# Strassen's multiplication, one level, for the gate and up products of four SwiGLU FFNs

## Chip, cores and metric

The kernel runs on one core of a Trainium2 chip. The metric is the device time of one execution in microseconds (us), read as the median of several runs. The engines have queues of their own: PE (TensorE, matrix products; PEld are its weight loads), DVE (VectorE), ACT (ScalarE), POOL (GpSimd), and SP (SyncE, which issues the DMAs of the weights). Each engine works its queue in order.

## The reference, cut

Two transformer blocks follow one another on 512 tokens of 1024 features, in float32. The second one has two layers, each with a SwiGLU FFN before its mixer and one behind it, so four in all, with 2816 hidden features (`D_FF`):

```python
def swiglu(h, w_gate, w_up, w_down):
    return (jax.nn.silu(h @ w_gate) * (h @ w_up)) @ w_down
...
    for layer in range(DEPTH):
...
        x = x + 0.5 * swiglu(rmsnorm_2(x, ffn1_norm[layer]), ffn1_w_gate[layer],
                             ffn1_w_up[layer], ffn1_w_down[layer])
...
        x = x + 0.5 * swiglu(rmsnorm_2(x, ffn2_norm[layer]), ffn2_w_gate[layer],
                             ffn2_w_up[layer], ffn2_w_down[layer])
```

## The kernel before

**Precision.** Every float32 factor is split into a high part (a copy to the matmul type) and a low part (the factor less its high part), and a product is three matmuls: high by high, high by low, low by high. Weights are split on the core: ACT writes the high part (line 78, tile `wh`), DVE the low one (line 79, `wl`). Activations are kept feature-major, `xT` [128, 8, 512], with the split parts `ah` and `al`.

**The four FFNs** are called "a", "b", "c", "d" here. Their hidden features are 22 chunks of 128. For a chunk m, the gate block (1024 x 128) is the stationary side in 8 pieces of 128x128, the tokens move: 8 x 3 matmuls of 512 columns (`fm`, lines 252, 254, 256), and the same for up. That makes 1056 such matmuls in an FFN. Then DVE multiplies both by `rB` (the norm's factor for each token, lines 394 and 396), ACT takes Silu (395), POOL multiplies (397), and `split` makes the parts `hh` (ACT, 237) and `hl` (DVE, 238). `rB` comes from a chain behind the first gate product (`stat1`, `stat2`; the matmuls of line 301, the copy of line 302).

**Down products** come in four groups of 6, 6, 5 and 5 chunks (`GROUPS`), each with 8 requests, one for each 128 output features: three matmuls of 512 columns for a chunk (lines 364 to 366), 528 in an FFN, and an addition to `xT` on DVE (369). A group is emitted behind the first chunk of the next group.

**The weights' queue** (`Stream`) is one list of requests for the whole kernel. SP loads a request into one of three staging tiles `ws`; when request i is fetched, the requests up to i + 2 are split, so that a weight's high and low parts are emitted two requests ahead of the matmuls that read them. The order of all work is that of emission.

Of the kernel before, what the change touches and what calls it, by code (L numbers as in the profile page):

```python
# [32 lines left out]

VECS = (
# [14 lines left out]
class Stream:  # L49
    def __init__(self, nc, pool, nst, nhl):  # L50
        self.nc, self.pool, self.nst, self.nhl = nc, pool, nst, nhl
        self.req, self.i, self.nd, self.ns = [], 0, 0, 0
        self.st, self.hl = {}, {}

    def add(self, key, ap, raw=False, use=None):
        """a request; its parts are high and low ones, or itself if raw, or what use(tile) makes of it."""
        self.req.append((key, ap, raw, use))

    def _dma(self, j):
        ap = self.req[j][1]  # L60
        a, b = ap.shape[1], ap.shape[2]
        t = self.pool.tile([P, 1024], F32, tag="ws", bufs=self.nst, name=f"ws{j}")
        v = t[:, :a * b].rearrange("p (a b) -> p a b", b=b)
        self.nc.sync.dma_start(v, ap)
        self.st[j] = (t, a, b)

    def _split(self, j):
        t, a, b = self.st.pop(j)
        n = a * b
        if self.req[j][3]:  # L70
            self.hl[j] = self.req[j][3](t[:, :n].rearrange("p (a b) -> p a b", b=b))
            return
        if self.req[j][2]:
            self.hl[j] = t[:, :n].rearrange("p (a b) -> p a b", b=b)
            return
        h = self.pool.tile([P, 1024], F32R, tag="wh", bufs=self.nhl, name=f"wh{j}")
        l = self.pool.tile([P, 1024], F32R, tag="wl", bufs=self.nhl, name=f"wl{j}")
        self.nc.scalar.activation(h[:, :n], t[:, :n], AF.Copy)  # L78
        self.nc.vector.tensor_tensor(l[:, :n], t[:, :n], h[:, :n], ALU.subtract)  # L79
        self.hl[j] = tuple(z[:, :n].rearrange("p (a b) -> p a b", b=b) for z in (h, l))  # L80
# [37 lines left out]
class Kernel:  # L118
    def __init__(self, tc, I, es):
# [94 lines left out]
    def vcols(self, first):  # L214
        """rows to columns: VC[:, i] is row i."""
# [27 lines left out]
    def fm(self, outs, w, x, nk=NK, k0=0, kw=0, first=True, last=True):  # L243
        """outs: [(psum AP, column slice of x)]; w: hi/lo [128, k, 128] stationary."""
# [13 lines left out]
    def fm_side(self, jobs, x, hook):  # L258
        """fm's side by side, chunk of x by chunk as they come, by parts of the tokens (the outs of a job)."""
# [7 lines left out]
    # ---- norms over the feature axis of a feature-major tensor  # L267
# [10 lines left out]
    def rcols(self, acc, nt, eps=EPS, dim=D, tag="M"):  # L278
        """acc [128, nt*128] per-partition partial sums of squares -> [128, nt] rsqrt columns."""
# [24 lines left out]
    # ---- block 2  # L304
# [17 lines left out]
    def feed(self, d, n, stats=True):  # L322
        """chunk n of x is final: its scaled hi/lo parts and its squares."""
# [15 lines left out]

    def plan_swiglu(self, key, wg, wu, wd):  # L340
        for gi, (m0, nm) in enumerate(GROUPS):
            for m in range(m0, m0 + nm):
                self.ws.add((key, "g", m), colblock(wg, m * P))
                self.ws.add((key, "u", m), colblock(wu, m * P))
                if m == m0 and gi:
                    self.plan_down(key, gi - 1, wd)
        self.plan_down(key, 3, wd)
# [8 lines left out]
    def down512(self, key, gi, hs, scale, on_x=None):  # L356
        nc = self.nc
        m0, nm = GROUPS[gi]
        for n in range(NK):
            wh, wl = self.ws.get((key, "d", gi, n))  # L360
            q = self.mps()
            for k in range(nm):
                hh, hl = hs[m0 + k]
                nc.tensor.matmul(q, wh[:, k], hh[:, :T], start=k == 0, stop=False)  # L364
                nc.tensor.matmul(q, wh[:, k], hl[:, :T], start=False, stop=False)  # L365
                nc.tensor.matmul(q, wl[:, k], hh[:, :T], start=False, stop=k == nm - 1)  # L366
            x = self.xT[:, n]
            s = scale if isinstance(scale, float) else scale(n)
            nc.vector.scalar_tensor_tensor(x, q, s, x, ALU.mult, ALU.add)  # L369
            if on_x is not None and gi == 3:  # L370
                on_x(n)

# [5 lines left out]
    def swiglu(self, key, d, on_x):  # L378
        nc = self.nc
        hs = {}  # L380
        sl = slice(0, T)
        for gi, (m0, nm) in enumerate(GROUPS):
            for m in range(m0, m0 + nm):
                q = self.dbl()
                w = self.ws.get((key, "g", m))
                self.fm([(q[:, 0], sl)], w, d.x)
                if d.rB is None:
                    self.stat1(d)
                w = self.ws.get((key, "u", m))
                self.fm([(q[:, 1], sl)], w, d.x)  # L390
                if d.rB is None:
                    self.stat2(d)
                a, b = self.tmp(T, tag="ta"), self.tmp(T, tag="tb")
                nc.vector.tensor_tensor(a, q[:, 0], d.rB, ALU.mult)  # L394
                nc.scalar.activation(a, a, AF.Silu)  # L395
                nc.vector.tensor_tensor(b, q[:, 1], d.rB, ALU.mult)
                nc.gpsimd.tensor_tensor(b, a, b, ALU.mult)  # L397
                hs[m] = self.htiles()
                self.split(hs[m][0], hs[m][1], b)
# [2069 lines left out]
```

## Time and profile before

| | us |
|---|---|
| median of 3 runs (3926.29 to 3926.95) | 3926.34 |
| span of the profiled execution, first to last instruction | 3923.9 |
| PE busy in it | 3757.1 |
| DVE busy in it | 2155.4 |
| ACT busy in it | 1375.5 |
| FFN "a", 1920.5 to 2297.4 | 376.9 |
| FFN "b", 2484.9 to 2860.6 | 375.7 |
| FFN "c", 2953.3 to 3326.6 | 373.3 |
| FFN "d", 3539.2 to 3912.5 | 373.3 |

The profile is of one execution, whose span is 2.4 us shorter than the median. An FFN's stretch runs from its first gate matmul to its last down matmul. Matmuls overlap in the records: the start of one to the start of the next is what it costs, and the duration shown is longer.

### The profile page before, as it was taken

To read this page: it belongs to the slowest core of one execution; us is meant where nothing else is said; L and a number is where in the kernel's file an instruction comes from. 1 tells how busy PE (TensorE), PEld (TensorE's weight loads), DVE (VectorE), ACT (ScalarE), POOL (GpSimd) and SP (SyncE) were. 2 spreads that over 40 slices of the span, in tenths; PEclk is the share of its full clock that TensorE was granted. 3 is DMA by queue.
4 is the path that set the end of the run, shared out by engine and by line. 5 is a ranking of instruction groups with operands and counts; after the bars stand their busy time and mean duration, and the time that the engine had idled before them with its cause. 6 is when DMAs were issued, how large, how long until landed. Compare 5 with 4: busy or idle time off the path is not lost.

```text
span 3923.9 us, 48420 instructions
## 1 busy us (share of the span) xinstructions
PE 3757.1 (96%) x18524; PEld 3101.1 (79%) x18524; DVE 2155.4 (55%) x3793; ACT 1375.5 (35%) x2306; POOL 833.5 (21%) x843
## 2 busy tenths in 40 slices
PE   8899999999999979999999998999999999899999
PEld 6887978888877778887788876888778887678887
DVE  8887787665555395444533358433463334764333
ACT  2454432121234384323322245322242223563222
POOL 6424230000021282000200035100030001451000
PEclk9999999999999999999999998999999999899999
DMA  6200043344413542333333322333253333213332
GB/s 189 90 1 22 20 127 117 118 123 123 123 49 103 161 111 69 95 97 89 84 97 89 94 67 79 94 93 92 86 157 97 93 93 101 89 46 92 92 95 86
DMA packets 583044, 367.27 MB, mean 94 GB/s; under 512 B 31415, under 2 KB 560301, under 8 KB 582813
## 3 DMA queue, kind: packets, MB, share of 16 engines
q1 hardware_dynamic: 561501, 348.30, 30.2%
q0 software_dynamic: 3520, 9.59, 0.8%
q10 hardware_dynamic: 17792, 6.29, 0.7%
q8 instruction: 147, 2.41, 0.3%
q14 instruction: 84, 0.69, 0.1%
HBM read 347.82 MB, written 16.30 MB: 93 GB/s over the span
## 4 chain that ended last, share of the span: by engine, by line
PE 75%; DVE 13%; ACT 4%; issue 4%; POOL 1%; DMA 1%; SPq 0%; POOLq 0%; DVEq 0%; ACTq 0%
PE D L252 10%; PE D L254 10%; PE D L256 10%; PE D L1252 6%; PE M L365 4%; PE M L366 4%; PE M L364 4%; PE E L252 3%; PE E L256 3%; PE E L254 3%; PE V L1697 2%; DVE wl L79 2%; PE M L252 2%; PE M L254 2%; PE M L256 2%
## 5 line engine op out<-in xcount | busy, mean ns | idle before, releaser
L79 DVE TENSOR_TENSOR wl<-ws,wh 128x1024 fp32r<-128x1024 f32 (+3 forms) x590 | 683.7, 1178 | 240.2 <-ACT wh L78 238.3
L78 ACT ACTIVATE wh<-ws 128x1024 fp32r<-128x1024 f32 (+3 forms) x590 | 534.8, 933 | 557.5 <-PE M L365 218.9
L252 PE MATMUL D<-ah,wh 128*128 128x512 f32 (+1 forms) x1384 | 550.3, 398 | 3.3 <-ACT wh L78 2.7
L256 PE MATMUL D<-ah,wl 128*128 128x512 f32 (+1 forms) x1384 | 547.1, 395 | 3.3 <-DVE wl L79 3.3
L254 PE MATMUL D<-al,wh 128*128 128x512 f32 (+1 forms) x1384 | 547.8, 396 | 1.1 <-POOL al L2391 0.6
L397 POOL TENSOR_TENSOR t<-t,t 128x512 f32<-128x512 f32 x88 | 113.4, 1289 | 1274.7 <-ACT t L395 1274.7
L252 PEld LDWEIGHTS D<-ah,wh 128*128 128x128 f32 x1384 | 262.1, 189 | 68.3 <-ACT wh L78 3.1
L256 PEld LDWEIGHTS D<-ah,wl 128*128 128x128 f32 x1384 | 261.9, 189 | 67.4 <-DVE wl L79 5.0
L254 PEld LDWEIGHTS D<-al,wh 128*128 128x128 f32 x1384 | 262.0, 189 | 66.4 <-issue 1.8
L364 PE MATMUL M<-hh,wh 128*128 128x512 f32 x704 | 279.7, 397 | 4.9 <-ACT hh L237 3.1
L365 PE MATMUL M<-hl,wh 128*128 128x512 f32 x704 | 279.5, 397 | 0.9 <-DVE hl L238 0.9
L366 PE MATMUL M<-hh,wl 128*128 128x512 f32 x704 | 279.0, 396 | 0.0
L395 ACT ACTIVATE t<-t 128x512 f32<-128x512 f32 x88 | 55.7, 633 | 619.2 <-DVE t L394 619.2
L238 POOL TENSOR_TENSOR hl<-t,hh 128x768 fp32r<-128x768 f32 (+1 forms) x44 | 69.2, 1574 | 806.6 <-ACT hh L237 766.0
L252 PE MATMUL E<-ah,wh 128*128 128x512 f32 x520 | 209.3, 402 | 6.6 <-DVE G L566 3.9
L256 PE MATMUL E<-ah,wl 128*128 128x512 f32 x520 | 209.1, 402 | 0.9 <-DVE wl L79 0.9
L254 PE MATMUL E<-al,wh 128*128 128x512 f32 x520 | 209.1, 402 | 0.3 <-DVE al L241 0.3
L394 DVE TENSOR_TENSOR t<-D,rB 128x512 f32<-128x512 f32 x58 | 40.1, 692 | 300.4 <-PE D L256 290.7
L1069 DVE SCALAR_TENSOR_TENSOR as<-ws,S,as 128x256 f32<-128x256 f32 x448 | 198.4, 496 | 5.6 <-DMA ws<-in_ada_w_dram 2.2
L369 DVE SCALAR_TENSOR_TENSOR xT<-M,xT 128x512 f32<-128x512 f32 x128 | 88.2, 689 | 203.6 <-PE M L366 203.3
L252 PE MATMUL D<-x7h,wh 128*128 128x512 f32 (+1 forms) x464 | 183.5, 398 | 2.5 <-ACT x7h L2386 1.6
L254 PE MATMUL D<-x7l,wh 128*128 128x512 f32 (+1 forms) x464 | 181.6, 394 | 0.6 <-DVE x7l L2393 0.5
(663 smaller groups left out, 8029.7 us busy)
## 6 DMA issues: line engine op xcount, KB each, us to landing
ws<-in_ffn_w_up_dram SPq DMA_DIRECT2D x176, 512.0 KB
ws<-in_ada_w_dram SPq DMA_DIRECT2D x88, 512.0 KB
ws<-in_ffn_w_gate_dram SPq DMA_DIRECT2D x88, 512.0 KB
ws<-in_ffn_w_down_dram SPq DMA_DIRECT2D x96, 384.0 KB
ws<-in_ffn_w_down_dram SPq DMA_DIRECT2D x96, 320.0 KB
ws<-in_ml_w_in_dram SPq DMA_DIRECT2D x24, 512.0 KB
ws<-in_rec_w_in_dram SPq DMA_DIRECT2D x16, 512.0 KB
mU<-Ud SPq DMA_DIRECT2D x8, 768.0 KB
```

What stands on the lines that cost most here:

```text
L78: self.nc.scalar.activation(h[:, :n], t[:, :n], AF.Copy)
L79: self.nc.vector.tensor_tensor(l[:, :n], t[:, :n], h[:, :n], ALU.subtract)
L252: nc.tensor.matmul(o, wh[:, kw + k], xh[:, k0 + k, s], start=a, stop=False)
L254: nc.tensor.matmul(o, wh[:, kw + k], xl[:, k0 + k, s], start=False, stop=False)
L256: nc.tensor.matmul(o, wl[:, kw + k], xh[:, k0 + k, s], start=False, stop=z)
L364: nc.tensor.matmul(q, wh[:, k], hh[:, :T], start=k == 0, stop=False)
L365: nc.tensor.matmul(q, wh[:, k], hl[:, :T], start=False, stop=False)
L366: nc.tensor.matmul(q, wl[:, k], hh[:, :T], start=False, stop=k == nm - 1)
L369: nc.vector.scalar_tensor_tensor(x, q, s, x, ALU.mult, ALU.add)
L397: nc.gpsimd.tensor_tensor(b, a, b, ALU.mult)
L1069: nc.vector.scalar_tensor_tensor(t, w[:, kk], c, t, ALU.mult, ALU.add)
L1252: nc.tensor.matmul(o, w[u][:, k], hs[m0 + k][h][:, s], start=k == 0 and i == 0, stop=k == nm - 1 and i == 2)
```

## The change

The hidden chunks are taken in 11 pairs. Pair 0 (chunks 0 and 1) keeps the form of before. For each of the other ten, the product of the pair's weights (256 hidden features, K = 1024 in two halves) with the tokens (two halves of 256) is a 2 x 2 block product, made by seven block products instead of eight: seven steps, each with 24 matmuls of 256 columns (gate and up, four pieces of K, three parts). The sums that this needs:

- of weights: four blocks (gate and up side by side, 1024 elements) are loaded, in two DMAs each, and four additions on DVE (`sw_step`, in place in the staging tiles) make the others; each of the seven operands is split, its high part by ACT and its low part by DVE. The low part is emitted later than before (`late`, `flush`): ahead of the next request's split, or at the end of the step.
- of activations: `x_sums`, four calls in an FFN, between the products of pair 0, on DVE and ACT.
- of results: each step's 512 columns in PSUM (gate and up) are copied by ACT (steps 0, 1, 2 and 6, lines 574 and 590) or combined by DVE (3, 4, 5), and at a pair's end `scaled`, `both` and `low` do what lines 394 to 397 and 237 to 238 did, in instructions of 1024 elements, with the multiplication on DVE instead of POOL. `scaled` follows step 6; `both` and `low` follow later steps, one each.

Down products have five groups (4, 4, 4, 4, 6 chunks; `PAIRS`), their requests lie one by one between the steps of the next two pairs, and their weights have staging tiles of their own (three, tag "ca").

```diff
+PAIRS = ((0, 2), (2, 2), (4, 2), (6, 2), (8, 3))
...
+    def parts(self, t, n, late=False):
+        h = self.pool.tile([P, 1024], F32R, tag="wh", bufs=self.nhl, name=f"wh{self.ns}")
+        l = self.pool.tile([P, 1024], F32R, tag="wl", bufs=self.nhl, name=f"wl{self.ns}")
         self.nc.scalar.activation(h[:, :n], t[:, :n], AF.Copy)
+        def low():
+            self.nc.vector.tensor_tensor(l[:, :n], t[:, :n], h[:, :n], ALU.subtract)
+        if late:
+            self.late.append(low)
+        else:
+            low()
+        return h, l
...
+    def sw_items():
+        for gi, (p0, n) in enumerate(PAIRS):
+            down = [("d", gi - 1, n) for n in range(NK)] if gi else []
+            for q in range(n):
+                if p0 + q == 0:
+                    for m in range(2):
+                        yield "g", 0, m
+                        yield "u", 0, m
+                    continue
+                for s in range(7):
+                    yield "s", p0 + q, s
+                    if down and s in ((2, 3, 5, 6), (1, 2, 4, 6))[q]:
+                        yield down.pop(0)
+            assert not down
+        for n in range(NK):
+            yield "d", len(PAIRS) - 1, n
...
+    def sw_blocks(ws, p, s):
+        if s > 3:
+            return None
+        i, k = ((0, 0), (1, 0), (1, 1), (0, 1))[s]
+        return [colblock(w[k * T:(k + 1) * T], (2 * p + i) * P) for w in ws]
+    def sw_step(self, key, p, s):
+        st = self.blocks.setdefault((key, p), [])
+        def use(t):
+            if t is not None:
+                st.append(t)
+            to, of = {1: (0, 1), 2: (0, 2), 4: (1, 2), 6: (3, 0)}.get(s, (None, None))
+            if to is not None:
+                self.nc.vector.tensor_tensor(st[to], st[to], st[of], ALU.add)
+            h, l = self.ws.parts(st[(0, 0, 0, 3, 1, 2, 3)[s]], 1024, True)
+            for i in {4: (1,), 5: (2,), 6: (0, 3)}.get(s, ()):
+                self.ws.free_late(st[i])
+            return tuple(z.rearrange("p (u k n) -> p u k n", u=2, n=P) for z in (h, l))
+        return use
...
+    def x_sums(self, d, n):
+        nc = self.nc
+        th, tl = (z[:, 2 * n:2 * n + 2].rearrange("p a b -> p (a b)") for z in d.t)
+        g, gb = (self.v(d.g[0], d.g[1] + i) for i in (n, n + 4))
+        ng = self.tmp(2, tag="mb", bufs=3)[:, 0:1]
+        a0, a1, b0, b1 = (self.xT[:, i, s] for i in (n, n + 4) for s in (slice(0, TC), slice(TC, T)))
+        f, e = (self.tmp(T, tag="ta")[:, :TC], self.tmp(T, tag="tb")[:, :TC])
+        t = self.tmp(TT, tag="ca", bufs=3)
+        nc.vector.tensor_scalar(ng, gb, -1.0, None, ALU.mult)
+        nc.vector.tensor_tensor(f, a0, a1, ALU.subtract)
+        nc.scalar.activation(e, a1, AF.Copy, scale=g)
+        nc.scalar.activation(f, f, AF.Copy, scale=g)
+        nc.scalar.activation(th[:, 0:TC], f, AF.Copy)
+        nc.vector.scalar_tensor_tensor(t[:, TC:2 * TC], b1, gb, e, ALU.mult, ALU.subtract)
+        nc.vector.scalar_tensor_tensor(t[:, 0:TC], b1, ng, f, ALU.mult, ALU.subtract)
+        nc.vector.scalar_tensor_tensor(t[:, 2 * TC:], b0, ng, t[:, 0:TC], ALU.mult, ALU.subtract)
+        nc.scalar.activation(th[:, TC:], t, AF.Copy)
+        nc.vector.tensor_tensor(tl[:, 0:TC], f, th[:, 0:TC], ALU.subtract)
+        nc.vector.tensor_tensor(tl[:, TC:], t, th[:, TC:], ALU.subtract)
...
+    def sw_first(self, key, d):
+        nc = self.nc
+        z, zf = self.hz(), self.gu()
+        for m in range(2):
+            q = self.dbl()
+            for i, kind in enumerate("gu"):
+                self.fm([(q[:, i], slice(0, T))], self.ws.get((key, kind, 0, m)), d.x)
                 if d.rB is None:
+                    (self.stat2 if i else self.stat1)(d)
+                if m == 0 and i == 0:
+                    d.t = self.acts512()
+                else:
+                    self.x_sums(d, 2 * m + i - 1)
+            nc.vector.tensor_tensor(zf[:, :, m], q, d.rB.unsqueeze(1).to_broadcast([P, 2, T]), ALU.mult)
+            nc.scalar.activation(zf[:, 0, m], zf[:, 0, m], AF.Silu)
+            nc.vector.tensor_tensor(zf[:, 1, m], zf[:, 0, m], zf[:, 1, m], ALU.mult)
+            nc.scalar.activation(z[:, 0, m], zf[:, 1, m], AF.Copy)
+            nc.vector.tensor_tensor(z[:, 1, m], zf[:, 1, m], z[:, 0, m], ALU.subtract)
+        self.x_sums(d, 3)
+        return z
...
-    def swiglu(self, key, d, on_x):
...
+    def swiglu(self, key, d, next_x):
+        nc = self.nc
+        self.ws.open([self.hp.tile([P, 1024], F32, name=self.nm("wz")) for i in range(2)])
+        hs, todo, un = {}, [], {}
+        lo, hi = slice(0, TC), slice(TC, T)
+        def product(q, w, x, k0, s, start, stop):
+            wh, wl = w
+            xh, xl = x
+            for u in range(2):
+                for k in range(4):
+                    o = q[:, u, lo]
+                    nc.tensor.matmul(o, wh[:, u, k], xh(k0 + k, s), start=start and k == 0, stop=False, skip_group_check=True)
+                    nc.tensor.matmul(o, wh[:, u, k], xl(k0 + k, s), start=False, stop=False, skip_group_check=True)
+                    nc.tensor.matmul(o, wl[:, u, k], xh(k0 + k, s), start=False, stop=stop and k == 3, skip_group_check=True)
+        def step(p, s, banks):
+            w = self.ws.get((key, "s", p, s))
+            if s == 0:
+                un[p] = dict(z=self.gu())
+            d_ = un[p]
+            r = banks[(0, 1, 0, 2, 0, 1, 0)[s]]
+            i = (None, 2, 1, None, 0, 3, None)[s]
+            if i is None:
+                k0, c = {0: (0, lo), 3: (4, lo), 6: (4, hi)}[s]
+                x = [lambda k, c, z=z: z[:, k, c] for z in d.x]
+            else:
+                k0, c = 0, slice(i * TC, (i + 1) * TC)
+                x = [lambda k, c, z=z: z[:, 2 * k:2 * k + 2].rearrange("p a b -> p (a b)")[:, c] for z in d.t]
+            product(r, w, x, k0, c, s in (0, 1, 3), s in (3, 5, 6))
+            if todo:
+                todo.pop(0)()
+            zf, q = d_["z"], r[:, :, lo]
+            def keep(name, tag):
+                d_[name] = t = self.tmp(T, tag=tag).rearrange("p (u s) -> p u s", u=2)
+                nc.scalar.activation(t, q, AF.Copy)
+            if s == 0:
+                keep("s", "sq")
+            elif s == 1:
+                keep("p", "ta")
+            elif s == 2:
+                keep("u", "tb")
+            elif s == 3:
+                nc.vector.tensor_tensor(zf[:, :, 0, lo], q, d_.pop("s"), ALU.add)
+            elif s == 4:
+                t = d_.pop("p")
+                for u in range(2):
+                    nc.vector.scalar_tensor_tensor(zf[:, u, 1, hi], q[:, u], -1.0, t[:, u], ALU.mult, ALU.subtract)
+            elif s == 5:
+                nc.vector.scalar_tensor_tensor(zf[:, :, 1, lo], q, -1.0, d_.pop("u"), ALU.mult, ALU.subtract)
+            else:
+                nc.scalar.activation(zf[:, :, 0, hi], q, AF.Copy)
+                todo.extend(end(p, zf))
+                todo.pop(0)()
+            self.ws.flush()
+        def end(p, zf):
+            rB = d.rB.unsqueeze(1).to_broadcast([P, 2, T])
+            def scaled():
+                for m in (1, 0):
+                    nc.vector.tensor_tensor(zf[:, :, m], zf[:, :, m], rB, ALU.mult)
+                    nc.scalar.activation(zf[:, 0, m], zf[:, 0, m], AF.Silu)
+            def both():
+                nc.vector.tensor_tensor(zf[:, 1], zf[:, 0], zf[:, 1], ALU.mult)
+                hs[p] = z = self.hz()
+                nc.scalar.activation(z[:, 0], zf[:, 1], AF.Copy)
+            def low():
+                nc.vector.tensor_tensor(hs[p][:, 1], zf[:, 1], hs[p][:, 0], ALU.subtract)
+            return scaled, both, low
+        items = list(self.sw_items())
+        last = len(PAIRS) - 1
+        on_x = None
+        for kind, a, b in items:
+            if kind == "g" and b == 0:
+                hs[0] = self.sw_first(key, d)
+                three = [self.bank("D"), self.bank("D"), self.bank("E")]
+            elif kind == "s":
+                if b == 0:
+                    three = three[2:] + three[:2]
+                step(a, b, three)
+            elif kind == "d":
+                if a == last and b == 0:
+                    while todo:
+                        todo.pop(0)()
+                    self.ws.flush()
+                    self.ws.close()
+                    on_x = next_x() if next_x else None
+                self.sw_down(key, a, b, hs, 0.5)
+                self.ws.flush()
+                if a == last and on_x:
+                    on_x(b)
```

The first place is DVE's queue in FFN "c" where pair 0 ends. Before, the evacuation of one chunk (394, 396, 238) stands between the splits of two weights:

```order
L394 TENSOR_TENSOR t_23886<-D_23825,rB_23811 128x512
L396 TENSOR_TENSOR t_23887<-D_23825,rB_23811 128x512
L238 TENSOR_TENSOR hl_23893<-t_23887,hh_23892 128x512
L79 TENSOR_TENSOR wl_23898<-ws_23785,wh_23897 128x1024
L79 TENSOR_TENSOR wl_23928<-ws_23830,wh_23927 128x1024
```

Now (515 is chunk 1's evacuation; 482 to 492 are `x_sums` for n = 3; `wl_25481` is the low part of pair 1's step 1):

```order
L515 TENSOR_TENSOR gu_25341<-D_25435,rB_25411 128x2x512
L517 TENSOR_TENSOR gu_25341<-gu_25341 128x512
L519 TENSOR_TENSOR hz_25340<-gu_25341,hz_25340 128x512
L482 TENSOR_SCALAR t_25527<-VC 128x1
L483 TENSOR_TENSOR t_25528<-xT 128x256
L487 SCALAR_TENSOR_TENSOR t_25530<-xT,VC,t_25529 128x256
L488 SCALAR_TENSOR_TENSOR t_25530<-xT,t_25527,t_25528 128x256
L489 SCALAR_TENSOR_TENSOR t_25530<-xT,t_25527,t_25530 128x256
L491 TENSOR_TENSOR al_25380<-t_25528,ah_25379 128x256
L492 TENSOR_TENSOR al_25380<-t_25530,ah_25379 128x768
L135 TENSOR_TENSOR wl_25481<-ws_72,wh_25480 128x1024
L454 TENSOR_TENSOR ws_72<-ws_72,wz_25339 128x1024
```

The low part of a weight now stands behind a chunk's evacuation and a whole call of `x_sums`.

The second place is DVE's queue in FFN "c" from the last evacuation of pair 3 (588) into pair 4 (600 is `scaled`, 604 `both`, 609 `low`; `wl_26339`, `wl_26373`, `wl_26392` are the low parts for steps 0, 1, 2 of pair 4; 534 adds a down product to `xT`):

```order
L588 SCALAR_TENSOR_TENSOR gu_26090<-D_25543,t_26197 128x2x256
L600 TENSOR_TENSOR gu_26090<-gu_26090,rB_25411 128x2x512 x2
L135 TENSOR_TENSOR wl_26339<-ws_72,wh_26338 128x1024
L454 TENSOR_TENSOR ws_72<-ws_72,wz_25338 128x1024
L534 SCALAR_TENSOR_TENSOR xT<-M_26375,xT 128x512
L135 TENSOR_TENSOR wl_26373<-ws_72,wh_26372 128x1024
L454 TENSOR_TENSOR ws_72<-ws_72,wz_25339 128x1024
L604 TENSOR_TENSOR gu_26090<-gu_26090 128x1024
L135 TENSOR_TENSOR wl_26392<-ws_72,wh_26391 128x1024
L135 TENSOR_TENSOR wl_26426<-t_26282,wh_26425 128x512
L609 TENSOR_TENSOR hz_26420<-gu_26090,hz_26420 128x1024
```

Both halves of `scaled` stand ahead of the low part of the next pair's step 0, and the addition for step 1 behind that. ACT's queue over the same stretch (132 are high parts, 590 the copy of step 6's result, 601 Silu, 606 the copy in `both`, 574 the copies of steps 0 to 2):

```order
L132 ACTIVATE wh_26338<-ws_72 128x1024
L590 ACTIVATE gu_26090<-D_25542 128x2x256
L601 ACTIVATE gu_26090<-gu_26090 128x512 x2
L132 ACTIVATE wh_26372<-ws_72 128x1024
L132 ACTIVATE wh_26391<-ws_72 128x1024
L606 ACTIVATE hz_26420<-gu_26090 128x1024
L574 ACTIVATE t_26422<-E_25544 128x512
L132 ACTIVATE wh_26425<-t_26282 128x512
```

The copy of step 0's result (574, from `E_25544`) stands behind the copy in `both` (606).

## Rows read from the trace of the kernel before

**Rows 1.** Span and mean granted clock of the core.

```profile
core 0: 3923.9 us, clock 0.983
```

**Rows 2.** Busy time by stretch: FFNs b and c, and 100 us within b.

```profile
2484.90:2860.60 375.70, 372.94 (x1591) 298.37 (x1590) 153.32 (x188) 107.09 (x141) 35.90 (x28) 1.00 0.31 91
2953.30:3326.60 373.30, 372.29 (x1587) 298.48 (x1586) 148.56 (x179) 103.05 (x135) 34.84 (x27) 1.00 0.32 93
...
2600.00:2700.00 100.00, 100.00 (x429) 80.38 (x428) 37.20 (x46) 25.17 (x32) 7.73 (x6) 1.00 0.32 94
```

**Rows 3.** Waits by engine, line and releaser (us, times, longest), FFN b.

```profile
ACT wh L78 <- DMA ws<-in_ffn_w_down_dram: 8.6, 3, 3.0
...
PE M L364 <- DVE xT L369: 1.7, 2, 0.9
```

**Rows 4.** PE's timeline, 256 columns: first and last of 48, twice.

```profile
583.62 0.28 PE L252 MATMUL M<-x7h,wh 128*128 128x256 f32 x1
...
588.96 0.28 PE L256 MATMUL A<-x7h,wl 128*128 128x256 f32 x1
...
1178.87 0.28 PE L252 MATMUL D<-x7h,wh 128*128 128x256 f32 x1
...
1184.40 0.28 PE L256 MATMUL D<-x7h,wl 128*128 128x256 f32 x1
```

**Rows 5.** Weight loads by line and form, 1178.8 to 1184.5 us.

```profile
L252 PEld LDWEIGHTS D<-x7h,wh 128*128 128x128 f32 x16 | 3.0, 188 | 0.0
```

**Rows 6.** By line and form in FFN b: busy us, mean ns | idle before.

```profile
L79 DVE TENSOR_TENSOR wl<-ws,wh 128x1024 fp32r<-128x1024 f32 x36 | 42.7, 1220 | 3.1 <-ACT wh L78 3.1
...
L78 ACT ACTIVATE wh<-ws 128x1024 fp32r<-128x1024 f32 x36 | 36.7, 1050 | 35.8 <-PE M L365 35.8
...
L395 ACT ACTIVATE t<-t 128x512 f32<-128x512 f32 x19 | 12.0, 633 | 141.3 <-DVE t L394 141.3
...
L394 DVE TENSOR_TENSOR t<-D,rB 128x512 f32<-128x512 f32 x12 | 8.3, 692 | 66.1 <-PE D L256 66.1
```

**Rows 7.** The same columns as in rows 6, instructions of 256 elements, whole span.

```profile
L2378 DVE SCALAR_TENSOR_TENSOR t<-xT,a,A 128x256 f32<-128x256 f32 x16 | 6.9, 473 | 0.0
L826 DVE TENSOR_TENSOR t<-dfQ,qr2C 128x256 f32<-128x256 f32 x16 | 6.6, 415 | 0.0
...
L2383 ACT ACTIVATE t<-t,ada 128x256 f32<-128x256 f32 x12 | 5.9, 495 | 0.0
```

**Rows 8.** DVE's and ACT's timelines in FFN b: start, duration, idle before.

```profile
2530.96 0.69 DVE L394 TENSOR_TENSOR t<-D,rB 128x512 f32<-128x512 f32 x1 [4.40 <-PE D L256]
2531.57 0.68 DVE L396 TENSOR_TENSOR t<-D,rB 128x512 f32<-128x512 f32 x1
...
2531.75 0.63 ACT L395 ACTIVATE t<-t 128x512 f32<-128x512 f32 x1 [6.63 <-DVE t L394]
```

**Rows 9.** The timeline where FFN b's factor rB is made.

```profile
2496.17 1.02 PE L301 MATMUL M<-t,ones 128*128 128x512 f32 x2
...
2497.22 0.60 ACT L302 ACTIVATE rB<-M 128x512 f32<-128x512 f32 x1 [8.90 <-PE M L301]
```

**Rows 10.** PE's timeline at the start of FFN b's last down group.

```profile
2831.35 0.40 PE L366 MATMUL M<-hh,wl 128*128 128x512 f32 x1
2832.53 0.49 PE L364 MATMUL M<-hh,wh 128*128 128x512 f32 x1 [0.78 <-ACT hh L237]
2833.25 0.50 PE L365 MATMUL M<-hl,wh 128*128 128x512 f32 x1 [0.23 <-DVE hl L238]
```

**Rows 11.** PE's timeline behind a wait, and busy time after it.

```profile
2370.07 0.51 PE L252 MATMUL E<-ah,wh 128*128 128x512 f32 x1 [1.97 <-ACT wh L78]
...
2371.56 0.80 PE L256 MATMUL E<-ah,wl 128*128 128x512 f32 x1 [0.55 <-DVE wl L79]
...
2377.27 0.41 PE L252 MATMUL E<-ah,wh 128*128 128x512 f32 x1
...
2371.50:2377.00 5.50, 5.44 (x13) 4.29 (x14) 4.50 (x7) 2.95 (x4) 2.23 (x4) 0.50 0.38 109
```

More of the change, by code (lines that the diff above doesn't have):

```diff
@@ L50, in __init__ @@
     def __init__(self, nc, pool, nst, nhl):
[L51 to L57, printed above, removed]
-    def _dma(self, j):
[L60 to L65, printed above, removed]
+        self.nc, self.pool, self.nhl = nc, pool, nhl
@@ new lines, in __init__, with add, _slot @@
+        self.slots = [pool.tile([P, 1024], F32, name=f"ws{i}") for i in range(nst)]
+        self.extra = []
+        self.req, self.i, self.nd, self.ns, self.ncol = [], 0, 0, 0, 0
+        self.st, self.hl, self.raws, self.late = {}, {}, [], []
+    def add(self, key, ap, raw=False, use=None, step=False, stage=None):
+        self.req.append((key, ap, raw, use, step, stage))
+    def _slot(self, step):
+        if self.slots:
+            return self.slots.pop(0)
+        return self.extra.pop(0) if step and self.extra else None
@@ L76, in _split @@
[L76 to L80 removed]
+        v = t[:, :n].rearrange("p (a b) -> p a b", b=b)
+        if use:
+            self.hl[j] = use(v)
+        elif raw:
+            self.hl[j] = v
+            self.raws.append((j, t))
+            return
+        else:
+            h, l = self.parts(t, n)
+            self.hl[j] = tuple(z[:, :n].rearrange("p (a b) -> p a b", b=b) for z in (h, l))
@@ L82, in spare, with free_late, flush @@
+    def free_late(self, t):
+        self.late.append(lambda: self.release(t))
+    def flush(self):
+        while self.late:
+            self.late.pop(0)()
     def spare(self, tag):
@@ L338, in stat2 @@
         self.rbcast(d.dg, 4, d.rB)
-    def plan_swiglu(self, key, wg, wu, wd):
[L341 to L347, printed above, removed]
+    @staticmethod
+    def sw_items():
[14 more added lines that the diff above has]
+            yield "d", len(PAIRS) - 1, n
@@ L354, in plan_down @@
                 self.plan_ada(ada)
[L356 to L371, printed above, removed]
     def htiles(self, w=T):
@@ L376, in htiles @@
                 self.hp.tile([P, w], F32R, tag="hl", bufs=n, name=self.nm("hl")))
-    def swiglu(self, key, d, on_x):
+    def x_sums(self, d, n):
         nc = self.nc
[L380 to L386, printed above, removed]
-                if d.rB is None:
[L388 to L399, printed above, removed]
-                if m == m0 and gi:
-                    self.down512(key, gi - 1, hs, 0.5)
-        self.down512(key, 3, hs, 0.5, on_x)
@@ new lines, in sw_down @@
+    def sw_down(self, key, gi, n, hs, scale):
+        nc = self.nc
+        p0, np_ = PAIRS[gi]
+        wh, wl = self.ws.get((key, "d", gi, n))
+        q = self.mps()
+        for k in range(2 * np_):
+            z, i = hs[p0 + k // 2], k % 2
+            nc.tensor.matmul(q, wh[:, k], z[:, 0, i], start=k == 0, stop=False)
+            nc.tensor.matmul(q, wh[:, k], z[:, 1, i], start=False, stop=False)
+            nc.tensor.matmul(q, wl[:, k], z[:, 0, i], start=False, stop=k == 2 * np_ - 1)
+        x = self.xT[:, n]
+        nc.vector.scalar_tensor_tensor(x, q, scale, x, ALU.mult, ALU.add)
@@ L1086, in ada @@
                 if j == m - 1:
[L1087 removed]
+                    sums = self.ap.tile([P, 256], F32, tag="arow", bufs=2, name=self.nm("arow"))
                     self.nc.scalar.activation(sums[0:2, :m * P], q, AF.Copy)
```

101 lines of the change are left out of this document (75 added, 26 removed).

## The prediction, made before the changed kernel had run

> **What bounds the kernel now.** I read the span and clock first, to see what fraction of the peak clock is granted: 0.983 over 3923.9 us, so the clock has little left to give [rows 1]. The busy times by stretch come next, because the change lives in the four FFNs alone: in FFN "c" PE is busy 372.3 of 373.3 us, DVE 148.6 and ACT 103.1; "b" is the same with 2.8 us of gaps [rows 2]. So an FFN is a stretch of matmuls without holes, and its time is their number times their spacing: 428 to 429 in 100 us, 233.6 ns each at clock 1.00 [rows 2]; (1056 + 528) x 0.2336 = 370.0 us. The waits confirm it: PE's own are 1.7 us for additions to xT [rows 3] and 0.78 and 0.23 us where the last down group starts [rows 10]; Off PE an instruction costs nothing as long as it comes two requests ahead. The question is thus how many matmul columns go, and whether DVE and ACT still stay ahead.
>
> **What PE saves.** A matmul of 256 columns stands in the trace twice in unbroken rows of 48: (1184.40 - 1178.87) / 47 = 117.7 ns, and (588.96 - 583.62) / 47 = 113.6 ns [rows 4]. The first writes one tile (D) all along, as a step does; the second writes two tiles in turn. I take 117.7 and keep 113.6 as a bound. Per FFN, gate and up were 1056 x 0.2336 = 246.7 us; now 96 x 0.2336 = 22.4 (pair 0) and 10 x 7 x 24 = 1680 x 0.1177 = 197.7. Saved: **26.5 us** (33.4 by the other row). The 528 down matmuls stay.
>
> The row shows 117.7 against 233.6 ns, a ratio of 2.0, so half the columns cost half the time [rows 2, 4]. The Trainium skill, page "TensorE: Matmul & The Clock Gate", section "Back-to-back issue gap", speaks against the change here: it gives a stream of weight load and matmul pairs about 81 ns at 128 columns and about 131 ns at 512. A straight line between, as an estimate from that page, makes 98 ns at 256 columns, and by it an FFN's gate and up products would go from 138 to 177 us, and the four FFNs would be about 155 us slower. The trace does not agree with that page at either width (233.6 and 117.7 ns).
>
> **What DVE and ACT get.** Durations: DVE 1024 elements 1.22 us, 512 0.69, ACT 1024 1.05, 512 0.63 [rows 6]; 256 elements 0.42 to 0.47 on DVE, 0.50 on ACT with a factor per partition [rows 7]; ACT from PSUM 0.60 [rows 9]; 768 elements, between 512 and 1024, about 0.95 and 0.84. On one engine the next starts about 0.08 before the last has ended (2531.57 against 2530.96 + 0.69), so in a row 1024 elements take 1.14 and 512 take 0.61; an engine follows another after 0.05 to 0.1 (2531.75 against 2531.65) [rows 8]. A pair with four downs is 7 x 24 x 0.1177 + 48 x 0.2336 = 31.0 us on PE. On DVE it is 7 low parts, 4 additions, and 4 instructions at the end, 15 x 1.14 = 17.1, four low parts and four additions for the downs 8 x 0.61 = 4.9, evacuations about 2: 24 us, 77%. So DVE does not become the bound by its sum. But it works in order, and at two places PE needs a low part that stands behind other work. I walked the queues there, row by row.
>
> *The start of an FFN*, from the end of the first up product on PE. rB comes at 1.7 (matmuls at 2496.17, its copy ends at 2497.82) [rows 9]. ACT's factors for the first `x_sums` stand behind that copy, and DVE behind them: its end is at 5.3. The evacuation of chunk 0 (1.22, Silu 0.63, 0.69, ACT 0.63, low 0.69, handoffs) ends at 9.3. A call of `x_sums` is a round trip to ACT and back (0.42, 0.50, 0.47 three times, ACT 0.84, DVE 0.42 and 0.95): about 3.9. So: second call 13.1, low part of pair 1's step 0 14.3, an addition 15.4, third call 20.1 (its ACT steps wait behind a high part), chunk 1 24.1, fourth call 27.8, low part of step 1 29.0. PE, never held, would have done rB's matmuls 0.9, chunk 1's products 48 x 0.2336 = 11.2, step 0 2.8 and two matmuls of step 1 at 15.2. It waits 1.9 at step 0, 3.3 and 8.6 in step 1, and 0.7 in step 2, where the next high and low part (ACT 1.05, DVE 1.22) follow: **+14.5 us**. Bounds: 0 if all that were done ahead of rB; 18 if ACT's queue held every call as it does the third (4.7 instead of 3.9, 4 x 0.8 = 3.2 more).
>
> *From pair to pair*, from the end of step 6 on PE. DVE and ACT: 0.2 to the copy of the result (by ACT, 0.60, since the second half of `scaled` needs it), then `scaled` 1.22, the low part for the next step 0: done at 3.2; PE has a down product (12 x 0.2336 = 2.8) and two matmuls and wants it at 3.05: 0.2. Then the addition 1.14, ACT's high part 1.05, the low part 1.22 with handoffs: 6.75 against PE's 6.05: 0.7. Into an even pair no down lies between steps 1 and 2: addition (7.8), `both` (9.0), its copy on ACT (10.1), and only then the copy that frees step 0's bank (10.6), while PE is there at 9.3: 1.3. Into an odd pair a down product covers that. Ahead of pair 2 there is no down: 2.7. Sum: 2.7 + 4 x 0.9 (pairs 3, 5, 7, 9) + 4 x 2.2 (4, 6, 8, 10) = **+15.1 us**. Bounds: 0 if the 0.2 us steps turn out shorter everywhere; 24 if each transition is as the first.
>
> *The tail.* Nothing lies between step 6 and the last downs' fifth chunk but 12 matmuls: copy, `scaled`, Silu, `both`, copy 1.05, low 1.22 leave waits of 2.3 and 1.0, where 0.94 and 0.49 stood (2832.53 - 2831.35 and 2833.25 - 2832.53, each less 0.23) [rows 10]: **+2.0** (0 to 3).
>
> *The clock.* After waits of 1.97 and 0.55 us the trace shows 13 matmuls in 5.5 us at clock 0.50, 1.2 GHz, up to 2377.27: about 2.5 us lost [rows 11]. The start's waits are longer, but part of the slowness lies under DVE's chain: 1.5. The tail's are of the size of that row: 0.5. **+2.0** (0 to 5).
>
> Costed at nothing: POOL's multiplication goes (it stands in DVE's sum as `both`). The 8 more down requests' splits and additions lie under a pair's 31.0 us of PE with the rest of DVE's 24; without that cover each would cost 2 x 0.61. The weights' bytes are the same, but 80 DMAs of half the size replace 40 for the blocks on SP's queue; what hides them is the staging ahead, and what it costs if that fails is a rival below.
>
> **Sum.** -26.5 + 14.5 + 15.1 + 2.0 + 2.0 = +7.1 us an FFN, four of them +28 us. On the profiled execution 3923.9 + 28 = 3952; the median stands 2.4 above the span: **3955 us**, 0.7% slower. A measurement of this kernel can tell about 0.2% (8 us) from no change.
>
> **Rivals.**
> - *The transitions don't wait* (faster). Their waits are 0.2, 0.7 and 1.3 us at the end of chains of five to eight instructions, so 10% shorter chains remove most of them. Against it: the order of the queues is fixed, and all durations are rows. Without the 15.1: 4 x -8.0 = -32, **3894 us**. It decides from 7.1 us less waiting in an FFN, half of the transitions' sum.
> - *The clock falls at the transitions too.* Into even pairs 2.2 us of waits lie within 8 us, as 2.5 lay within 4 in the row [rows 11]; 4 x 4 x 2.5 = +40: **3995 us**. Against it: 0.94 and 0.49 in the tail of "b" did not lower it, spacing after them stays near 0.23, and the stretch has clock 1.00 [rows 2, 10].
> - *256 columns at 113.6 ns* [rows 4]. 6.9 us more saved an FFN, of which three steps in seven lie ahead of a wait and give it back: 3.9 x 4 = 16: **3939 us**.
> - *Weights come late.* Staging tiles free up later (a block is held until its last sum), and ACT already waits up to 3.0 us for a load, three times in "b" [rows 3]. One such wait a pair reaching PE: 40 x 3.0 = +120, **4075 us**. For it: few tiles; against it: the queues of DMA are busy 31% [rows 2].
> - *Weight loads set the pace.* A load's record is 188 ns [rows 5], longer than 117.7. If a step ran at it, 1680 x 0.070 x 4 = +473: **4427 us**. Against it: the 48 in a row had a load each [rows 4, 5]. The Trainium skill's section named above points this way, since it has the load and the matmul set the spacing together; the trace does not show that at 256 columns.
>
> **Chances.** Forecast 0.43 (own range 3932 to 3975; 0.07 of it within 0.2%), transitions free 0.28, clock 0.11, 113.6 ns 0.10 (0.06 of it within 0.2%), late weights 0.05, load-bound 0.03. Faster 0.28; same 0.07 + 0.06 = 0.13; slower 0.36 + 0.04 + 0.11 + 0.05 + 0.03 = 0.59. The range, 3880 to 3996, leaves out the last two and the ends of the second and third, under 0.2 in all.
>
> **What would show it.** In the changed profile: steps of 24 matmuls in 2.8 us; PE waits in step 1 of pair 1 for `wl` (line 135) of 8 us and for `al`; 0.2 to 1.3 us waits at the first three steps of each pair, on `wl` and on line 574's copy; a clock below 1.00 only behind an FFN's start. I am wrong if the FFNs are shorter than 373 us, if PE waits at the transitions for nothing, or if the waits name a DMA.

## The result and the profile after

The changed kernel takes 3973.24 us (median of 4 runs, 3971.57 to 3975.06) against 3926.32 before: a ratio of 1.0121, 95% interval 1.0106 to 1.0135, so 47 us or 1.2% slower. The forecast was 3955 with the range 3880 to 3996, slower. The profiled execution spans 3973.3 us, 49.4 more than the one of before.

Where the 49.4 us lie is read from one matmul that both kernels have, the one that makes rB in FFN "a" (PE's timeline: start, duration, idle before). Before, and then after:

```profile
1933.76 2.08 PE L301 MATMUL M<-t,ones 128*128 128x512 f32 x2 [3.30 <-DVE t L295]
```

```profile
1949.12 2.07 PE L366 MATMUL M<-t,ones 128*128 128x512 f32 x2 [3.56 <-DVE t L360]
```

The changed kernel is 15.4 us late before its first Strassen step. From rB to the last down matmul the four FFNs took 363.6, 364.5, 362.0 and 362.0 us before, and 372.0, 370.6, 373.2 and 371.8 after: 35.5 more in all. What lies between them gives 1.5 back. From the first gate matmul itself the FFNs take 391.1, 382.7, 384.4 and 383.9 us after and 382.7, 376.6, 373.3 and 374.2 before (in the table of before, the stretches of "a", "b" and "d" begin 0.8 to 5.8 us behind that matmul).

FFN "c" after (PE, PEld, DVE, ACT, POOL busy; granted clock, DMA share, GB/s). This row begins at rB, 11.2 us behind the first gate matmul with which the row of "c" in [rows 2] begins; that both are 373.3 long is chance:

```profile
2992.00:3365.30 373.30, 346.85 (x2259) 313.91 (x2259) 275.97 (x310) 158.73 (x217) 7.81 (x6) 0.97 0.31 89
```

PE is busy 26 us less than its stretch, DVE 74% of it. PE's waits in the same stretch, of the kind shown for "b" in [rows 3] (us in total, times, longest; idle of 0.15 us and less is not listed):

```profile
PE D L551 <- DVE wl L135: 13.3, 7, 10.3
PE E L551 <- DVE wl L135: 4.3, 4, 1.9
PE D L549 <- ACT t L574: 3.5, 3, 1.2
PE E L549 <- ACT t L574: 2.4, 2, 1.2
PE M L530 <- ACT hz L606: 2.2, 1, 2.2
PE M L531 <- DVE hz L609: 0.5, 1, 0.5
```

No wait names a DMA. Low parts of weights come late (10.3 and 1.9 at the start, the others at the pairs), and line 574's copies. The longest stands in step 1 of pair 1, as forecast, but as one wait of 10.3 for `wl`; the walk had 3.3 for `al` and 8.6 for `wl` there, and PE waits for no `al`. In FFN "b" the same delay of the start is booked elsewhere, on a PSUM bank that chunk 1 still held:

```profile
PE E L549 <- DVE gu L515: 9.4, 1, 9.4
```

PE's timeline into pair 4 of FFN "b" shows the steps and the even pair's waits:

```profile
2634.25 0.28 PE L549 MATMUL D<-ah,wh 128*128 128x256 f32 x1
2634.37 0.28 PE L550 MATMUL D<-al,wh 128*128 128x256 f32 x1
2635.17 0.39 PE L551 MATMUL D<-ah,wl 128*128 128x256 f32 x1 [0.52 <-DVE wl L135]
2635.39 0.28 PE L549 MATMUL D<-ah,wh 128*128 128x256 f32 x1
...
2637.74 0.28 PE L551 MATMUL D<-ah,wl 128*128 128x256 f32 x1
2639.20 0.39 PE L549 MATMUL E<-ah,wh 128*128 128x256 f32 x1 [1.18 <-ACT t L574]
2639.42 0.28 PE L550 MATMUL E<-al,wh 128*128 128x256 f32 x1
```

Spacing in a step is (2637.74 - 2635.39) / 20 = 117.5 ns. The idle in brackets counts from the modelled end of the matmul before; from start to start the first wait costs 2635.17 - 2634.37 - 0.12 = 0.68 us and the second 1.34. The next matmul then also comes late: 0.22 instead of 0.12.

The granted clock in FFN "c", by stretch (start, transitions between pairs, tail):

```profile
3009.00:3021.00 12.00, 2.12 (x14) 1.92 (x13) 8.98 (x16) 5.28 (x10) 0.00 (x0) 0.64 0.00 0
3021.00:3031.00 10.00, 9.56 (x59) 9.56 (x60) 6.42 (x6) 5.47 (x7) 0.00 (x0) 0.70 0.00 0
...
3041.00:3100.00 59.00, 55.98 (x386) 51.34 (x385) 44.10 (x49) 25.42 (x35) 0.00 (x0) 1.00 0.30 87
...
3200.00:3330.00 130.00, 124.26 (x866) 114.17 (x864) 100.49 (x108) 54.21 (x73) 0.00 (x0) 1.00 0.30 85
3330.00:3345.00 15.00, 13.59 (x45) 10.57 (x46) 7.85 (x9) 5.59 (x8) 1.34 (x1) 0.77 0.18 52
```

It falls behind the start's and the tail's waits and is 1.00 through the transitions, also behind the longest, into pair 2, with two waits 4 us apart:

```profile
3045.32 0.39 PE L551 MATMUL E<-ah,wl 128*128 128x256 f32 x1 [1.36 <-DVE wl L135]
3049.29 0.40 PE L549 MATMUL D<-ah,wh 128*128 128x256 f32 x1 [1.12 <-ACT t L574]
```

### The profile page after: what moved, and what is told of

Read it like the earlier page. It is cut to its first block, busy times and chain, and to the rows that moved or that the text cites. A ratio compares the mean times of both kernels' runs of the same rounds, so it can differ in the third digit from the quotient of the medians.

```text
span 3973.3 us, 55166 instructions
## 1 busy us (share of the span) xinstructions
PE 3694.2 (93%) x21404; PEld 3198.1 (80%) x21404; DVE 2670.4 (67%) x4329; ACT 1604.9 (40%) x2642; POOL 720.0 (18%) x755
## 4 chain that ended last, share of the span: by engine, by line
PE 64%; DVE 19%; ACT 7%; issue 6%; DMA 3%; POOL 1%; SPq 0%; DVEq 0%; ACTq 0%; POOLq 0%
PE D L1483 6%; PE D L317 5%; PE D L319 5%; PE D L321 5%; DVE wl L135 5%; PE D L551 3%; PE D L549 3%; PE D L550 3%; PE M L531 3%; PE M L532 3%; PE M L530 3%; PE V L1928 2%; DVE ws L454 2%; ACT wh L132 2%; PE E L549 2%
## 5 line engine op out<-in xcount | busy, mean ns | idle before, releaser
L551 PE MATMUL D<-ah,wl 128*128 128x256 f32 x1440 | 411.2, 286 | 48.9 <-DVE wl L135 48.0
L549 PE MATMUL D<-ah,wh 128*128 128x256 f32 x1440 | 407.3, 283 | 13.8 <-ACT t L574 13.8
L550 PE MATMUL D<-al,wh 128*128 128x256 f32 x1440 | 405.6, 282 | 0.0
L530 PE MATMUL M<-hz,wh 128*128 128x512 f32 x704 | 282.3, 401 | 8.6 <-ACT hz L606 8.6
L531 PE MATMUL M<-hz,wh 128*128 128x512 f32 x704 | 282.5, 401 | 2.7 <-DVE hz L609 2.7
L532 PE MATMUL M<-hz,wl 128*128 128x512 f32 x704 | 281.8, 400 | 0.0
L549 PE MATMUL E<-ah,wh 128*128 128x256 f32 x800 | 227.2, 284 | 19.2 <-ACT t L574 9.7
L551 PE MATMUL E<-ah,wl 128*128 128x256 f32 x800 | 229.0, 286 | 14.1 <-DVE wl L135 13.5
L317 PE MATMUL D<-ah,wh 128*128 128x512 f32 (+1 forms) x512 | 205.8, 402 | 6.4 <-DVE G L797 4.2
L321 PE MATMUL D<-ah,wl 128*128 128x512 f32 (+1 forms) x512 | 203.9, 398 | 2.5 <-DVE wl L135 2.5
L319 PE MATMUL D<-al,wh 128*128 128x512 f32 (+1 forms) x512 | 203.7, 398 | 0.3 <-POOL al L2625 0.2
```

The source lines that it names most:

```text
L317: nc.tensor.matmul(o, wh[:, kw + k], xh[:, k0 + k, s], start=a, stop=False)
L319: nc.tensor.matmul(o, wh[:, kw + k], xl[:, k0 + k, s], start=False, stop=False)
L321: nc.tensor.matmul(o, wl[:, kw + k], xh[:, k0 + k, s], start=False, stop=z)
L530: nc.tensor.matmul(q, wh[:, k], z[:, 0, i], start=k == 0, stop=False)
L531: nc.tensor.matmul(q, wh[:, k], z[:, 1, i], start=False, stop=False)
L532: nc.tensor.matmul(q, wl[:, k], z[:, 0, i], start=False, stop=k == 2 * np_ - 1)
```

## The experiments

Four questions: is the loss ahead of FFN "a" the staging of weights; are the waits from pair to pair a matter of order in the queues, or is DVE short of time; is the start the queue of `x_sums`; and does the saving appear once the waits are gone.

**Staging tiles in rotation outside the FFNs.** The changed kernel takes the tile that was released first, the kernel before took the three in turn.

```diff
+        if not step and not self.extras:
+            t = self.ring[0]
+            if not any(t is z for z in self.slots):
+                return None
+            self.slots = [z for z in self.slots if z is not t]
+            self.ring.append(self.ring.pop(0))
+            return t
         if self.slots:
```

> The changed kernel, with its three staging tiles handed out in strict rotation outside the FFNs, as before. If the 15 us that the changed kernel loses ahead of the first SwiGLU FFN come from the way in which tiles are handed out (the tile released first, so that two loads can follow one another into one tile), they go: 3973 - 13 to 15 = 3958 to 3960 us, and the FFNs keep their 371 to 373 us from rB to the last down product. If they come from anything else (a later start, another placement in memory, more code), the time stays at 3973 +- 3 us.

Measured: 3958.92 us (3958.51 to 3959.86), ratio to before 1.0080 (1.0065 to 1.0095). rB of FFN "a" is back at its place, within 0.8 us:

```profile
1934.51 2.07 PE L376 MATMUL M<-t,ones 128*128 128x512 f32 x2 [3.41 <-DVE t L370]
```

**The new staging alone**, in the kernel before (its `Stream` replaced, nothing else).

> The kernel before, with only the changed kernel's staging put in (tiles handed out as they are released); no Strassen step. If the staging alone costs the 14 us outside the FFNs, 3926 + 13 to 15 = 3940 us; inside the FFNs, where one weight follows the other, nothing. If the loss outside needs the FFNs' change, 3926 +- 3 us.

Measured: 3943.06 us (3940.67 to 3945.34), ratio 1.0039 (1.0024 to 1.0054), against 3930.02 for the kernel before beside it: +13. Its FFNs take 363.5, 364.5, 362.0 and 362.0 us, as before; rB of "a" is 11.7 us late:

```profile
1945.46 2.08 PE L363 MATMUL M<-t,ones 128*128 128x512 f32 x2 [3.29 <-DVE t L357]
```

So the 14 us outside the FFNs are the staging. Matched matmul by matmul, this run is 7.7 us behind the kernel before at 170 us, 10.1 at 580 and 12.0 at 1461. The largest place is at the very start of the kernel. SP's timeline before, then in the changed kernel (two loads in one row):

```profile
56.67 7.10 SPq L64 DMA_DIRECT2D ws<-in_att_w_in_dram  x2
```

```profile
57.21 12.15 SPq L102 DMA_DIRECT2D ws<-in_att_w_in_dram  x2
```

In the changed kernel the two loads go into the same tile: the second is held on SP until DVE has made the low part of the first (SP's waits, 55 to 72 us).

```profile
SPq L102 <- DVE wl L135: 6.3, 1, 6.3
```

ACT then waits for that load, in the stretch from 55 to 80 us, before and after:

```profile
ACT wh L78 <- DMA ws<-in_att_w_in_dram: 3.3, 1, 3.3
```

```profile
ACT wh L132 <- DMA ws<-in_att_w_in_dram: 13.0, 2, 11.0
```

**Four portions at a pair's end instead of three**, each behind the step's own copy out of PSUM.

```diff
-            if todo:
-                todo.pop(0)()
             zf, q = d_["z"], r[:, :, lo]
...
                 todo.extend(end(p, zf))
-                todo.pop(0)()
+            if todo:
+                todo.pop(0)()
             self.ws.flush()
...
-            def scaled():
-                for m in (1, 0):
-                    nc.vector.tensor_tensor(zf[:, :, m], zf[:, :, m], rB, ALU.mult)
-                    nc.scalar.activation(zf[:, 0, m], zf[:, 0, m], AF.Silu)
+            def scaled(m):
+                nc.vector.tensor_tensor(zf[:, :, m], zf[:, :, m], rB, ALU.mult)
+                nc.scalar.activation(zf[:, 0, m], zf[:, 0, m], AF.Silu)
...
-            return scaled, both, low
+            return lambda: scaled(1), lambda: scaled(0), both, low
```

> The changed kernel, with the work at a pair's end in four portions instead of three (second half of scaled behind step 6, first half behind the next step 0, both behind step 1, low behind step 2), each behind the step's own copy out of PSUM. If the waits from pair to pair come from the place of this work in DVE's and ACT's queues (walked: 15.1 us an FFN, 0.7 left with this order), 4 x 14 = 56 us go, and some of the lowered clock with them: 3973 - 56 to 68 = 3905 to 3917 us. If DVE is short of time as such (busy 75% of an FFN), the waits only move, and the time falls by less than 15 us: over 3958.

Measured: 3911.82 us (3909.07 to 3913.88), ratio 0.9958 (0.9941 to 0.9974), as expected of the order in the queues. PE's waits in FFN "c":

```profile
PE D L551 <- DVE wl L135: 10.9, 2, 10.6
PE M L530 <- ACT hz L604: 2.2, 1, 2.2
PE E L551 <- DVE wl L135: 2.0, 1, 2.0
PE M L531 <- DVE hz L607: 0.8, 1, 0.8
```

All waits between pairs but one of 0.3 us are gone, the start's and the tail's stay. No work was taken off DVE.

**The same edit with three portions** (`scaled`'s first half and `both` together).

```diff
+            def scaled(m=1):
+                nc.vector.tensor_tensor(zf[:, :, m], zf[:, :, m], rB, ALU.mult)
+                nc.scalar.activation(zf[:, 0, m], zf[:, 0, m], AF.Silu)
             def both():
+                scaled(0)
```

> As the run with four portions, but with three: second half of scaled behind step 6, first half and both in one portion behind the next step 0, low behind step 1. The walk of the queues says that this takes the waits away at steps 0 and 1 and at step 0's copy, and makes new ones at step 2, whose low part stands behind the Silu's round trip and both: 2.5, 0.5 and 1.85 us, 12.6 us an FFN in place of 15.1 : 3973 - 4 x 2.3 = 3964 us. If what matters is only that step 0's copy stands ahead and that scaled is halved, this run is as good as the one with four portions: 3905 to 3917 us.

Measured: 3970.85 us (3965.43 to 3973.42), ratio 1.0108 (1.0093 to 1.0123): no gain that the runs can tell. In FFN "c":

```profile
PE D L551 <- DVE wl L135: 18.0, 7, 10.5
PE E L551 <- DVE wl L135: 6.1, 4, 1.9
```

Line 574 has left the list, and `wl` has grown instead, from 17.6 to 24.1: the wait moved from the copy to step 2's low part. There PE loses 2.6, 0.6 and 2.0 us from start to start (into pair 2, the odd and the even pairs), where 2.5, 0.5 and 1.85 were walked. The time is 7 us above the 3964 all the same, because the clock falls more often. The wait into pair 2, now 2.4 us in one piece, lowers it in all four FFNs; here in "c":

```profile
3046.00:3052.00 6.00, 5.67 (x29) 5.41 (x30) 3.33 (x5) 3.29 (x6) 0.00 (x0) 0.72 0.45 132
```

One more slot in the order is worth 59 us, lowered clock included.

**An earlier start of `x_sums`.** Each call one product earlier, the first ahead of rB's copy on ACT; the second half of chunk 1's evacuation behind pair 1's steps 0 and 1.

```diff
-                if m == 0 and i == 0:
-                    d.t = self.acts512()
-                else:
-                    self.x_sums(d, 2 * m + i - 1)
+                if m == 0 and i == 0:
+                    self.stat1(d)
+                    d.t = self.acts512()
+                self.x_sums(d, 2 * m + i)
+                if m == 0 and i == 1:
+                    self.stat2(d)
...
+            if m:
+                todo.extend((both, low))
```

> The changed kernel, with each call of x_sums one gate or up product earlier (the first one behind the first gate product, so ahead of the copy that makes rB on ACT), and the second half of chunk 1's evacuation (multiplication, split) put behind the steps 0 and 1 of pair 1. If the start's wait is the queue of x_sums and evacuations on DVE, walked at 14.4 us, it shrinks to 4.3 (step 1's low part still behind the fourth call and chunk 1's first instruction); 4 x 10 = 40 us go, with up to 2 us of lowered clock in each FFN: 3973 - 40 to 48 = 3925 to 3933 us. If step 1's additions of weights or their loads set the start, it stays within 10 us of 3973.

Measured: 3950.63 us (3947.74 to 3954.57), ratio 1.0058 (1.0043 to 1.0074): 23 us gained, not 40. The expectation missed on two counts. FFN "b" still waits 9.6 us (from start to start) at step 0 for chunk 1's bank, which the walk did not hold. And the walk let `x_sums` begin long before rB; in FFN "c" it cannot, since DVE's queue there stands behind a high part that ACT makes only when it is through with the keys' work. The next run has the same start; DVE's and ACT's timelines in it:

```profile
2932.38 1.06 ACT L142 ACTIVATE wh<-ws 128x1024 fp32r<-128x1024 f32 x1 [0.46 <-ACT kvn L990]
```

```profile
2933.47 1.22 DVE L145 TENSOR_TENSOR wl<-ws,wh 128x1024 fp32r<-128x1024 f32 x1 [11.67 <-ACT wh L142]
...
2935.21 0.15 DVE L492 TENSOR_SCALAR t<-VC 128x1 f32<-128x1 f32 x1
```

DVE stood idle 11.67 us, and the first call began at 2935.21, 5 us ahead of rB.

**All three together** (rotation, four portions, earlier start).

> Rotation outside the FFNs, the earlier x_sums and the four portions at a pair's end, all in one kernel. If the three causes are separate and the 256-column steps save what their spacing says, the walk leaves 8.3 us of waits in an FFN instead of 32: 4 x 24 = 96 us, 14 us outside, about 2.5 us of restarts behind each FFN's 20 waits, and 1 to 3 us of clock: 3973 - 96 - 14 - 10 - 8 = 3845 us (3838 to 3860), faster than the kernel before by 2%. If DVE or ACT become the bound once the waits are gone, or the clock falls for another reason, over 3870 us.

Measured: 3875.48 us (3870.69 to 3878.79), ratio 0.9865 (0.9850 to 0.9880). Faster than before by 1.3%, but 15 us above the expected range, and so among the times that the expectation gave to a bound by DVE or ACT or to the clock. The start's remaining waits and the clock behind them are the larger part: 46 us of waits in the four FFNs (10.1 to 13.6 in each), where 33 were walked, and about 19 us of lowered clock, hardly less than the changed kernel's 20. That DVE is not the bound the next two runs show, which are faster with its work left as it is.

**The tail**: in the last down group, the first two requests' chunks of pairs 8 and 9 ahead of those of pair 10.

```diff
+        some(0, range(n4))
+        ws.append(self.ws.get((key, "d", gi, 1), held=1))
+        qs.append(self.mps())
+        some(1, range(n4))
+        for n in range(2):
+            some(n, range(n4, 2 * np_))
```

> As the run with all three, and in the last down group the first two requests' four chunks of pairs 8 and 9 ahead of the chunks of pair 10, so that 24 matmuls of 512 columns (5.6 us) instead of 12 cover the end of pair 10. If the tail's waits (2.3 and 1.0 us in the trace of the changed kernel) are that chain alone, 3 us an FFN go: 12 us less than the run with all three. If something else is late there, the two are equal within 3 us.

Measured: 3855.29 us (3853.25 to 3858.88), ratio 0.9818 (0.9801 to 0.9834): 20 us less, more than the 12 expected. The two waits shrink to one of 0.4 us in FFN "c", and the clock no longer falls behind them. Busy time at that place in the run without this edit and with it:

```profile
3256.00:3259.00 3.00, 2.98 (x7) 2.43 (x8) 1.28 (x2) 0.00 (x0) 0.00 (x0) 0.50 0.28 81
```

```profile
3250.00:3256.00 6.00, 6.00 (x28) 4.80 (x27) 3.67 (x4) 3.77 (x6) 1.84 (x2) 1.00 0.92 296
```

**The start again**: `x_sums` two calls side by side, all four ahead of rB's copy, both chunks' second halves put off.

```diff
+    def x_sums(self, d, *ns):
+        parts = [self.x_sum(d, n) for n in ns]
+        for _ in range(3):
+            for p in parts:
+                next(p)
...
-                self.x_sums(d, 2 * m + i)
+                if m == 0:
+                    self.x_sums(d, 2 * i, 2 * i + 1)
```

> As the run with the tail's change, with the calls of x_sums made two by two (DVE works on one while ACT has the other), both pairs ahead of rB's copy, and the second half of both chunks' evacuations behind the steps 0 and 1 of pair 1. If what remains at an FFN's start (7.3 to 10.6 us of waits, mostly step 1's low part, and 2 to 2.5 us of clock 0.5 behind them) is the round trips between DVE and ACT in x_sums and the evacuations on DVE's queue, all but about 1.5 us of the waits goes and the clock hardly falls: 4 x 8 to 11 = 32 to 44 us less than 3855: 3811 to 3823 us. If the start is held by the additions and splits of pair 1's weights, which stay as they are, the time falls by less than 15 us.

Measured: 3828.77 us (3826.72 to 3832.05), ratio 0.9744 (0.9728 to 0.9760). 26 us less than the run before it, short of the expected 32 to 44, but far over the 15 by which the weights of pair 1 would have shown as the cause. FFN "c" then waits 1.0 us in all:

```profile
PE M L575 <- DVE hz L657: 0.4, 1, 0.4
PE D L601 <- DVE wl L145: 0.3, 1, 0.3
PE E L601 <- DVE wl L145: 0.3, 1, 0.3
```

PE is busy through that stretch again, at full clock, beside a DVE that is busy 80% of it:

```profile
2918.00:3255.50 337.50, 336.31 (x2262) 306.57 (x2261) 271.05 (x301) 154.36 (x211) 7.80 (x6) 1.00 0.34 98
```

What is left lies in FFN "b" (3.5 us for chunk 1's bank) and FFN "a" (1.9 for a high part). This version beats both kernels: 2.6% under the one before.

## Why the prediction was right, and where it was off

The direction and the order of size hold, by the mechanism that the prediction gave. Its terms against the runs:

- **Saving, 26.5 us an FFN**: right. Within the steps, matmuls of 256 columns come every 117.5 to 117.7 ns on average, in all four FFNs. It is neither 113.6 ns nor the 188 of a weight load. The trace does not agree with the 98 ns estimated from the Trainium skill, page "TensorE: Matmul & The Clock Gate", section "Back-to-back issue gap". The saving shows as such in the last run, whose FFNs take 1357.8 us from rB to the end instead of 1452.1: 94 of the 4 x 26.5 = 106 us.
- **Waits, 14.5 + 15.1 + 3.4 us**: 33.0 forecast, 30.6 to 32.7 measured from start to start. Into pair 4 of "b" the walk gave 0.7 and 1.3, the rows above 0.68 and 1.34. At the start it gave 14.5, and 12 to 14 came. The rival of free transitions falls with them: what was fixed by the order of the queues came as walked. In "b" the start's wait stood at a bank instead of a low part, with the same size.
- **DVE is not the bound by its sum**: right, shown by the four portions, which took the waits away and left DVE's work as it was.
- **Clock, 2.0 us**: too small. Matmuls at lowered clock cost some 3 to 7 us an FFN, 20 in all (before: 0 to 2). I took 1.5 of the 2.5 us of one fall at the start and a fifth of one in the tail; FFN "c" has two at the start, 15 and 24 matmuls long, and one in the tail, 11 long.
- **The matmul after a wait** was not costed: some 2.5 to 3 us an FFN, 0.1 us behind each of about 26 waits (of these, the ones of 0.2 us from start to start are too short for the lists above).
- **"The change lives in the four FFNs alone"** is the step that failed. The diff also replaced the rule by which staging tiles are handed out, for the whole kernel. Ahead of FFN "a" the order of instructions is the same in both kernels; the tiles that the loads go to are not. That is 13 to 14 us of the 47, shown from both sides by the first two runs.

The sum after the fact, four FFNs: -106 saved, waits +125 less 8 before, restarts +11, clock +16: +38, against 35.5 measured from rB to the last down matmul. With 14 outside that makes 52 against 49.4. The forecast of 28 had most of the terms inside the FFNs and nothing outside. Inside it came within 8 us partly by luck: the waits were 7 us less than forecast, which covers part of the 8 more for the clock and the 11 for the matmuls after waits. The rival of late weights, which put waits for loads into the FFNs, is out, since PE has none there. The other clock rival is out for this kernel: 1.00 through all transitions. What it feared is real for longer waits, as the run with three portions shows.

What stays open: the changed staging wasn't taken apart load by load (the place at 57 us explains some 8 of its 13 to 14 us). In the last run, the pairing of `x_sums` and the put-off evacuations were not tried one without the other. Nothing was tried on the 4 to 5 us of waits that "a" and "b" keep in it.

## What to carry over

Where engines work queues in order, walk the queue of the helping engine with durations from the trace: busy shares of 75% say nothing on whether an operand two requests ahead is in time, while the walk gave the waits from pair to pair to about a tenth of a us, and an order that removes them. At the FFN's start it was up to 2.5 us off, and for the earlier start it left out a bank and a queue that was still held. A cheaper product pays only once the work that it needs beside it has left the places ahead of the next operand: the same arithmetic ran 1.2% slower or 2.6% faster, by its order and, for 14 of the 144 us between, by the tiles that the loads take. And a change of a shared helper counts everywhere: the same instructions into other buffers cost 13 us here.

## What was not expected of the hardware

A wait of PE costs more than its length: in the rows above the matmul after it comes 0.22 us later instead of 0.12, and behind the start's long wait in FFN "c" the clock fell to 1.2 GHz for 24 matmuls (2.3 us more). Which waits lower the clock was not plain from their sum (all from start to start). Waits of 0.2, 0.7 and 1.3 us within 8 us left it at 1.00, and so did 1.5 and 1.3 us into pair 2 of "c", 4 us apart. One wait of 2.6 us in the run with three portions lowered it in all four FFNs, and of the 16 of 2.0 us there one did. The tail's 2.3 and 1.0 us lowered it in every FFN of the changed kernel, and with one of 0.5 us in their place it stayed.
